# A hybrid decoder trunk: the first output projection by token tiles with resident weights, in place of block products

## The chip, the cores and the metric

The kernel runs on one core of one Trainium2 chip. The core has five engines that work side by side: TensorE (PE, with its weight loads as PEld), VectorE (DVE), ScalarE (ACT), GpSimd (POOL) and SyncE (SP, which here issues every DMA). The metric is the device time of one execution in microseconds (us), lower is better.

## The reference

Two layers on x of 2048 tokens by 1024 features, all float32. What matters here is the end of the first layer and the start of the second:

```python
def rmsnorm(x, g):
    y = x * lax.rsqrt(jnp.mean(x * x, axis=-1, keepdims=True) + RMS_EPS)
    return y * g

# layer 0, its end: eight heads (four softmax with forgetting, four stick-breaking)
mixed = concatenate([fox, sb], axis=-1) * silu(gate)      # 2048 x 1024
x1 = x + mixed @ even_w_out                               # 1024 x 1024 weights
# layer 1, its start
h = rmsnorm(x1, odd_norm)
proj = h @ odd_w_in                                       # q, k, v of three head groups, gate
```

`mixed @ even_w_out` is the first output projection. Layer 1 goes on with windowed attention in three groups of strides and a second output projection (`out = x1 + mixed1 @ odd_w_out`), which the change doesn't touch.

## The kernel before

Every product keeps nearly float32 accuracy by splitting both operands into a high half (rounded) and a low half, and by three matmuls: high by high, high by low, low by high (`mm3`, lines 88 to 93). The helper `split` makes the halves: high by a copy on ACT (line 81), low by a subtraction on DVE or POOL (line 86).

The large projections run as **block products** (`panel_steps`, line 261): for a panel of 512 columns and a half of the tokens (1024), the operands are cut into 2 by 2 blocks of 512, and seven products of sums of blocks take the place of eight products of blocks. One product is 48 matmuls of 128x256, in two halves, each with its own weight tile `wop`. `Weights` (line 184) makes these tiles a little ahead: it loads `wraw` (line 216), forms the block sums on POOL (line 226), and splits them (pool `wp`, 4 buffers). `left` (line 342) makes the seven left operands A11, A12, S2, S3, S1, A22, S4 of a token half from a transposed matrix in DRAM (`stage` and `lp` tiles, sums on DVE and POOL at line 345, splits); they live in the pool `big`, 8 buffers of 16 KB per partition. The results of the products are combined on DVE (line 300) and given to an `emit` function.

In the first output projection, four panels (two token halves by two column halves) are done so, from `mixT` (the transposed output of the attention). Its `emit` is `residual` (line 947): it loads a piece of x, adds (line 954), and stores to `x1d` in DRAM. Then, tile by tile (128 tokens), `transpose_to` (line 153) loads x1 again (`xt`), normalises it on ACT (squares at 131, scale at 133, with the small root steps at lines 104 to 114), transposes it on PE (line 142, 8 matmuls), scales by the norm's weights while copying out of PSUM (`te`, line 149, ACT), and stores to `hT1`, from which `left` makes the operands of layer 1. Transposes of the first token half are spread over the products of the second half, those of the second half over the first panels of layer 1 (`tick`).

The order of instructions on each engine isn't written out by hand: a scheduler orders them by priority (the order in which the program issues them) and by when it expects operands and buffers to be there. Each engine, and SP with its DMAs, then works through its queue in that order and stops at the first instruction whose operands aren't ready. The attention of layer 0 ends with eight units of 256 queries of the last head; a function `tail` is called between them, so that early work of the next stage can be laid beside them.

Of the kernel before, what the change touches and what calls it, by code (L numbers as in the profile page):

```python
# [8 lines left out]
F32 = mybir.dt.float32  # L9
# [551 lines left out]
def each(emit):  # L561

    def run(block, half, cs):
        for g, c in enumerate(cs):
            emit(block, half, g, c)
    return run
# [200 lines left out]
def even_attention(k, tail):  # L767
# [135 lines left out]
    for n, (kind, h, u) in enumerate(units):  # L903
# [20 lines left out]
        if nxt == len(order) and u in (5, 6):  # L924

            tail()
    for v in past:
        merged((pv(*v[0], v[1]), 1))


def odd_layer(k, x, x1, even_w_out, w_in, w_out, out):
# [4 lines left out]
    outs = [(even_w_out, plain(n * CH)) for n in range(2)]  # L936
    rounds = [[(n, g) for g in gs for n in "qkv"] + [("gate", 0)] for gs in ((1, 0, 2), (2, 1, 0))]
    cols = lambda n, g: plain(3 * 1536 if n == "gate" else "qkv".index(n) * 1536 + g * 512)
    W = Weights(k, outs * 2 + [(w_in, cols(*j)) for js in rounds for j in js],
                [2, 2] + [2, 1, 1, 1, 1, 1, 1, 1, 1] * 2)  # L940
    A = []
    lefts = left(k, k.mixT, 0, A)
    yield W, lefts

    tick = Pace()

    def residual(r, n):
        def emit(block, half, g, src):
            t0 = r * ROUND + block * CH + g * 256
            c0 = n * CH + half * 256  # L950
            view = lambda d: d[t0:t0 + 256, c0:c0 + 256].rearrange("(r p) c -> p r c", p=P)
            a = c2([P, 2, 256], name="x1t")
            nc.sync.dma_start(a, view(x))
            nc.vector.tensor_tensor(a, src.rearrange("p (r c) -> p r c", r=2), a, op=OP.add)
            nc.sync.dma_start(view(x1), a)
        return each(emit)
# [11 lines left out]

    for r in range(2):
        B = []  # L970
        nxt = left(k, k.mixT, 1, B) if r == 0 else left(k, T, 0, B)
        if r == 0:
            pace = Pace()
            pace.every = 2
            pace.add(lefts)
        both = two(A, [residual(r, n) for n in range(2)], pace if r == 0 else tick,
                   lambda j: None if j in EARLY else next(nxt))
        next(both)
        if r == 0:
            pace.finish()  # L980
            next(nxt)
            next(nxt)
        next(both)
        if r == 1:
            tick.finish()
            next(nxt)
            next(nxt)
        next(both)
        A = B
        tick.every = 1 if r == 0 else 4  # L990
        tick.add(iter("-"), staggered([k.transpose_to(T, x1, r * 8 + t, k.go) for t in (4, 5, 6, 7, 0, 1, 2, 3)]))
# [33 lines left out]

    box = k.big([P, 4, HG, 2, P], F32R, name="box")
    bias = box[:, 0].bitcast(F32)
    values = [box[:, 3].bitcast(F32).rearrange("p a b c -> p (a b c)")[:, i * HW:(i + 1) * HW] for i in range(4)]
    values += [k.hs.tile([P, HW], F32, name=f"v{i}") for i in range(2)]
    ring = box[:, 1:3].rearrange("p x a b c -> p (x a b c)").rearrange("p (z h s t) -> p z h s t", z=2, h=2, s=4)  # L1030
    pairs = box[:, 1:3].rearrange("p x a b c -> p (x a b c)").rearrange("p (z s h e t) -> p z s h e t", z=2, s=2, h=2, e=2)
# [153 lines left out]
    for r in range(2):  # L1185
        B = []
        nxt = left(k, T, 1, B, False)
        for i, (name, grp) in enumerate(rounds[r]):
# [11 lines left out]
            if i < 2:  # L1200
                if i == 0:
                    both = two(A, [emitter(r, *rounds[r][n]) for n in range(2)], beat)
                    next(both)
                next(both)
            else:
                panel(k, A, W, "t", emitter(r, name, grp), beat, (lambda j: next(nxt)) if last else None)
            if r == 0 and i == 2:
                tick.finish()
# [88 lines left out]
def tile_hybrid_trunk(ctx, tc, x, even_norm, even_w_in, even_b_f, even_q_gain, even_k_gain, even_w_out,  # L1297
# [12 lines left out]
    W, first = next(odd)  # L1310

    def tail():
        W.ahead(1)
        next(first)

    even_attention(k, tail)
    k.table()
# [29 lines left out]
```

## Time and profile before

| what | value |
|---|---|
| time, median of 3 runs | 2823.95 us (2823.14 to 2828.58) |
| the profiled execution's own time | 2826.53 us |
| its span in the trace | 2824.8 us |
| granted TensorE clock, mean | 0.979 |
| busy share of PE, DVE, ACT, POOL | 95%, 73%, 57%, 43% |
| last score product of layer 0's attention | 1283.0 us |
| matmuls of the projection, first to last start | 1297.4 to 1507.15 us |
| first matmul of layer 1's first panel | 1517.77 us |

In rows of groups the columns are: line, engine, operation, output<-inputs, shapes, count, then busy us, mean ns of one, and the idle time of the engine just before them with what ended it. Rows of the timeline give the start and the length in us, and in brackets the idle time before and its releaser. Lengths of matmuls include their pipeline, so that the step from start to start is the price of one. Rows of waits give the total in us, the number of times and the longest.

### The profile page before, as it was taken

Reading aid. Unit: us, or ns where it says so; the run is one execution under the profiler, and the core shown is the slowest. Engines: PE = TensorE matmul, PEld = TensorE weight load, DVE = VectorE, ACT = ScalarE, POOL = GpSimd, SP = SyncE. Lnnn points to the kernel's source line nnn. Section 1 sums busy time; section 2 is a strip of 40 time slices with the busy share of each in tenths; the row PEclk is TensorE's granted clock in tenths of the full one; section 3 lists DMA queues with packets and bytes.
Section 4 is the critical chain, followed back from the end, with each engine's and each line's share of the span. In section 5 each row is a group of like instructions: output and inputs, shape, how many; then the busy total and the mean of one; then the engine's idle time right before and its main releaser. Section 6 shows DMA issues by size and latency. Waiting matters only on the chain.

```text
span 2824.8 us, 55621 instructions
## 1 busy us (share of the span) xinstructions
PE 2676.4 (95%) x20191; PEld 2455.5 (87%) x20191; DVE 2052.7 (73%) x4373; ACT 1618.6 (57%) x3924; POOL 1223.4 (43%) x981
## 2 busy tenths in 40 slices
PE   6999999999999999998987999999989999999998
PEld 5898878998787789987887999999889999999876
DVE  7857684684888888888959857476797686763966
ACT  6465553454776666665364555555664577665642
POOL 3545464544544433326545544343245432422322
PEclk9999999999999999999998999999999999999999
DMA  5576544445433344435577553334543445444675
GB/s 180 181 222 210 172 160 154 154 142 192 144 111 118 112 123 144 139 104 173 187 232 246 154 179 107 121 122 146 169 128 126 139 140 166 132 147 134 219 254 183
DMA packets 398770, 449.43 MB, mean 159 GB/s; under 512 B 31712, under 2 KB 331040, under 8 KB 398496
## 3 DMA queue, kind: packets, MB, share of 16 engines
q1 hardware_dynamic: 398496, 445.89, 49.4%
q8 instruction: 159, 2.61, 0.4%
q14 instruction: 115, 0.94, 0.1%
HBM read 291.22 MB, written 154.57 MB: 158 GB/s over the span
## 4 chain that ended last, share of the span: by engine, by line
PE 62%; DVE 21%; DMA 7%; ACT 5%; issue 3%; POOL 1%; SPq 1%; DVEq 0%; ACTq 0%; POOLq 0%
PE ps L91 17%; PE ps L93 17%; PE ps L92 17%; DVE rest L828 4%; PE ps L863 2%; PE ps L1145 2%; DVE wop L86 2%; DVE A L86 2%; PE ps L1135 2%; PE ps L1116 2%; DVE lp L345 1%; DVE S L86 1%; PE ps L1061 1%; DVE pT L86 1%; DVE c L300 1%
## 5 line engine op out<-in xcount | busy, mean ns | idle before, releaser
L226 POOL TENSOR_TENSOR wraw<-wraw 128x512 f32<-128x512 f32 (+1 forms) x320 | 444.2, 1400 | 430.3 <-DVE wop L86 157.1
L81 ACT ACTIVATE wop<-wraw 128x512 fp32r<-128x512 f32 (+1 forms) x560 | 349.5, 629 | 383.4 <-PE ps L93 294.2
L86 POOL TENSOR_TENSOR wop<-wraw,wop 128x512 fp32r<-128x512 f32 (+1 forms) x240 | 329.4, 1375 | 534.0 <-ACT wop L81 503.8
L92 PE MATMUL ps<-wop,S 128*128 128x256 f32 (+1 forms) x1792 | 512.4, 286 | 18.1 <-DVE wop L86 16.8
L91 PE MATMUL ps<-wop,A 128*128 128x256 f32 (+1 forms) x1792 | 512.0, 287 | 14.2 <-DVE c L300 13.5
L91 PE MATMUL ps<-wop,S 128*128 128x256 f32 (+1 forms) x1792 | 515.8, 289 | 9.9 <-DVE c L300 6.3
L92 PE MATMUL ps<-wop,A 128*128 128x256 f32 (+1 forms) x1792 | 511.7, 286 | 2.2 <-DVE wop L86 1.5
L93 PE MATMUL ps<-wop,S 128*128 128x256 f32 (+1 forms) x1792 | 512.9, 287 | 0.0
L93 PE MATMUL ps<-wop,A 128*128 128x256 f32 (+1 forms) x1792 | 509.5, 285 | 0.0
L86 DVE TENSOR_TENSOR wop<-wraw,wop 128x512 fp32r<-128x512 f32 (+1 forms) x320 | 270.2, 845 | 232.0 <-ACT wop L81 230.6
L92 PEld LDWEIGHTS ps<-wop,S 128*128 128x128 f32 x1792 | 343.3, 192 | 21.0 <-DVE wop L86 17.8
L91 PEld LDWEIGHTS ps<-wop,A 128*128 128x128 f32 x1792 | 342.3, 191 | 19.0 <-issue 13.4
L91 PEld LDWEIGHTS ps<-wop,S 128*128 128x128 f32 x1792 | 342.1, 191 | 15.1 <-issue 8.4
L92 PEld LDWEIGHTS ps<-wop,A 128*128 128x128 f32 x1792 | 342.9, 191 | 4.0 <-DVE wop L86 3.2
L93 PEld LDWEIGHTS ps<-wop,S 128*128 128x128 f32 x1792 | 342.7, 191 | 3.3 <-issue 2.6
L93 PEld LDWEIGHTS ps<-wop,A 128*128 128x128 f32 x1792 | 342.7, 191 | 1.4 <-issue 0.8
L300 DVE TENSOR_TENSOR c<-u,ps 128x512 f32<-128x512 f32 (+1 forms) x274 | 178.7, 659 | 91.9 <-PE ps L93 86.1
L81 ACT ACTIVATE pT<-ps 128x512 fp32r<-128x512 f32 (+2 forms) x352 | 165.5, 504 | 135.6 <-PE ps L863 81.3
L831 POOL TENSOR_TENSOR rows<-rows,rest 128x512 f32<-128x512 f32 (+4 forms) x160 | 152.6, 957 | 162.1 <-DVE rest L828 141.8
L86 DVE TENSOR_TENSOR pT<-ps,pT 128x512 fp32r<-128x512 f32 (+2 forms) x352 | 188.0, 559 | 44.2 <-ACT pT L81 42.8
L1128 ACT ACTIVATE row<-row,nm 128x256 f32<-128x256 f32 (+1 forms) x384 | 172.5, 452 | 64.4 <-DVE nm L1126 63.9
L92 PE MATMUL ps<-pT,vt 128*128 128x256 f32 x576 | 171.1, 299 | 5.5 <-DVE pT L86 5.3
(214 smaller groups left out, 6485.0 us busy)
## 6 DMA issues: line engine op xcount, KB each, us to landing
wraw<-in_odd_w_in_dram SPq DMA_DIRECT2D x88, 512.0 KB, 4.0
wraw<-in_even_w_in_dram SPq DMA_DIRECT2D x70, 512.0 KB, 4.2
ld<-qk SPq DMA_DIRECT2D x106, 256.0 KB, 3.2
qk<-c SPq DMA_DIRECT2D x96, 256.0 KB, 2.4
lp<-hT SPq DMA_DIRECT2D x60, 256.0 KB, 3.6
uu<-ot SPq DMA_DIRECT2D x96, 132.0 KB, 1.9
fin<-uu SPq DMA_DIRECT2D x16, 792.0 KB, 4.5
hT<-te SPq DMA_DIRECT2D x48, 256.0 KB, 4.3
```

Source lines behind the costliest of these rows:

```text
L81: nc.scalar.activation(hi, src, AF.Copy)
L86: (nc.vector if lo_on == "dve" else nc.gpsimd).tensor_tensor(lo, src, hi.bitcast(F32), op=OP.subtract)
L91: mm(out, a[0], b[0], start=start, stop=False, skip_group_check=more)
L92: mm(out, a[0], b[1], start=False, stop=False, skip_group_check=more)
L93: mm(out, a[1], b[0], start=False, stop=stop, skip_group_check=more)
L226: tt = lambda e, o, x, y, op, s: e.tensor_tensor(o[:, s], x[:, s], y[:, s], op=op)
L300: nc.vector.tensor_tensor(out[g], x[g], y[g], op=OP.add)
L828: nc.vector.tensor_tensor_scan(o[:, b:b + n][:, ::-1], back, k.ident[:, :1].to_broadcast([P, n]), 1.0 if carry is None else carry, OP.mult ...
L831: nc.gpsimd.tensor_tensor(dst[:, :w], dst[:, :w], o[:, b + 1:b + 1 + w], op=OP.mult)
L863: nc.tensor.transpose(pt[:, (jx * 2 + i) * P:(jx * 2 + i + 1) * P], rows[:, i, (jj * 2 + jx) * P:(jj * 2 + jx + 1) * P], k.ident)
L1116: nc.tensor.matmul(scores(hp, e), q[pr, za, hp], ring[pr, zb, hp, blocks], start=i == 0, stop=i == 2)
L1128: nc.scalar.activation(row[:, h // 2, h % 2, :nk], row[:, h // 2, h % 2, :nk], AF.Exp, bias=nm[:, h:h + 1], accum_out=ot[:, HW + HG + h:HW ...
```

## The change

The first output projection no longer uses block products. A new function `first_out` keeps all of `even_w_out` on the chip as halves: four tiles `wo` in the pool `big`, loaded before the attention and split between the last units of its last head. It then takes pairs of token tiles from `mixT`, splits them (`ml`, also in `big`), and goes through 16 token tiles one by one: load x (`xt`), for each column half 8 x 3 matmuls of 128x512 into one PSUM bank and the sum with x in place, store to x1, normalise the same tile in place, transpose, store to `hT1`. Three tiles are in flight in a stagger. x1 is no longer read back for the norm. The left operands of layer 1's first half are begun near the end of the tiles (steps 13 and 14); the rest of them is issued with layer 1's first products. `box`, a tile of layer 1's attention, is made later, since its buffer isn't free before. `k.table()` behind the attention is gone.

```diff
-        if nxt == len(order) and u in (5, 6):
+        if nxt == len(order) and u in (3, 4, 5, 7):
             tail()
     for v in past:
         merged((pv(*v[0], v[1]), 1))
+        tail()
+
+def first_out(k, x, x1, w, T, W, lefts):
+    nc = k.nc
+    wo, raws, ml = {}, {}, {}
+    quarters = [(n, z) for n in range(2) for z in range(2)]
+
+    def load(i):
+        n, z = quarters[i]
+        raws[i] = [k.raws.tile([P, 2, CH], F32, name="wraw", tag="raw") for _ in range(2)]
+        for j, raw in enumerate(raws[i]):
+            k0 = (z * 4 + j * 2) * P
+            nc.sync.dma_start(raw, w[k0:k0 + 2 * P, n * CH:(n + 1) * CH].rearrange("(k p) n -> p k n", p=P))
+
+    def quarter(i):
+        t = wo[quarters[i]] = k.big([P, 4, 2, CH], F32R, name="wo")
+        for j, raw in enumerate(raws.pop(i)):
+            k.split(t[:, 2 * j:2 * j + 2, 0], t[:, 2 * j:2 * j + 2, 1], raw, "act", "dve")
+
+    def mixed(b):
+        t = ml[b] = k.big([P, KT, 2, 2 * P], F32R, name="ml")
+        for j in range(4):
+            c = k.c2([P, 2, 2 * P], name="mp", tag="res")
+            nc.sync.dma_start(c, k.mixT[:, 2 * j:2 * j + 2, b * 2 * P:(b + 1) * 2 * P])
+            k.split(t[:, 2 * j:2 * j + 2, 0], t[:, 2 * j:2 * j + 2, 1], c, "act", "dve")
+
+    def rows(t):
+        xt = k.w4([P, D], name="xt")
+        nc.sync.dma_start(xt, x[t * P:(t + 1) * P, :])
+        yield
+        m, i = ml[t // 2], slice(t % 2 * P, (t % 2 + 1) * P)
+        for n in range(2):
+            acc = k.ps("s")
+            for kk in range(KT):
+                k.mm3(acc, [m[:, kk, z, i] for z in range(2)],
+                      [wo[n, kk // 4][:, kk % 4, z] for z in range(2)], kk == 0, kk == KT - 1)
+            half = xt[:, n * CH:(n + 1) * CH]
+            nc.vector.tensor_tensor(half, acc, half, op=OP.add)
+        nc.sync.dma_start(x1[t * P:(t + 1) * P, :], xt)
+        k.normalise(xt)
+        yield
+        k.transposed(xt, k.go, lambda z: k.c2([P, 4, P], name="te"),
+                     lambda z, d: nc.sync.dma_start(T[:, z * 4:(z + 1) * 4, t * P:(t + 1) * P], d))
...
+    steps = staggered(rows(t) for t in range(NTT))
...
+    for s in range(NTT + 2):
+        next(steps, None)
+        if s in (2, 4, 6, 8, 10, 12):
+            mixed(s // 2 + 1)
+        if s == 9:
+            W.ahead(1)
+        if s in (13, 14):
+            next(lefts)
...
-    W = Weights(k, outs * 2 + [(w_in, cols(*j)) for js in rounds for j in js],
-                [2, 2] + [2, 1, 1, 1, 1, 1, 1, 1, 1] * 2)
+    W = Weights(k, [(w_in, cols(*j)) for js in rounds for j in js], [2, 1, 1, 1, 1, 1, 1, 1, 1] * 2)
     A = []
-    lefts = left(k, k.mixT, 0, A)
-    yield W, lefts
+    lefts = left(k, T, 0, A)
+    yield from first_out(k, x, x1, even_w_out, T, W, lefts)
     tick = Pace()
+    tick.add(lefts)
...
-        both = two(A, [residual(r, n) for n in range(2)], pace if r == 0 else tick,
-                   lambda j: None if j in EARLY else next(nxt))
...
-        tick.add(iter("-"), staggered([k.transpose_to(T, x1, r * 8 + t, k.go) for t in (4, 5, 6, 7, 0, 1, 2, 3)]))
```

The scheduler orders anew around the change. On PE, at the end of the attention (`ps<-pT,vt` is its value product, `ps<-ident,rows` its transposes), the order before is:

```order
L863 MATMUL ps<-ident,rows 128x128 x13
L91 MATMUL ps<-pT,vt 128x256
L91 MATMUL ps<-wop,A_14733 128x256
L92 MATMUL ps<-wop,A_14733 128x256
L93 MATMUL ps<-wop,A_14733 128x256
```

and now, at the same place:

```order
L863 MATMUL ps<-ident,rows 128x128 x9
L91 MATMUL ps<-pT,vt 128x128
L91 MATMUL ps<-pT,vt 128x256
L91 MATMUL ps<-wo,ml 128x512
L92 MATMUL ps<-wo,ml 128x512
```

In both, matmuls of the projection stand among the last value products; now they are those of the first two token tiles. On PE at the start of layer 1, the order before goes from the last block product of the projection straight to layer 1's first operand (`A_17358` is A11 of layer 1), with the tile transposes elsewhere:

```order
L91 MATMUL ps<-wop,S_16413 128x256
L92 MATMUL ps<-wop,S_16413 128x256
L93 MATMUL ps<-wop,S_16413 128x256
L91 MATMUL ps<-wop,A_17358 128x256
L92 MATMUL ps<-wop,A_17358 128x256
```

Now the last token tile is followed by the same product, with the transposes of tile 14 one matmul behind its start:

```order
L92 MATMUL ps<-wo,ml 128x512
L93 MATMUL ps<-wo,ml 128x512
L91 MATMUL ps<-wop,A_16626 128x256
L142 MATMUL ps<-ident,xt 128x128 x8
L92 MATMUL ps<-wop,A_16626 128x256
```

Those of each earlier tile stand a whole tile's matmuls behind its own, those of tile 15 at the end of the third product of layer 1. On DVE at that place, layer 1's operands stood before among residual adds (L954), block sums (L300) and weight halves:

```order
L86 TENSOR_TENSOR S_17538<-stage,S_17538 128x512 x2
L954 TENSOR_TENSOR x1t<-c,x1t 128x512
L300 TENSOR_TENSOR c<-u_17376,ps 128x512
L954 TENSOR_TENSOR x1t<-c,x1t 128x512
L345 TENSOR_TENSOR lp<-lp,stage 128x512
L954 TENSOR_TENSOR x1t<-c,x1t 128x512
L345 TENSOR_TENSOR lp<-lp 128x512
L300 TENSOR_TENSOR c<-u,ps 128x512 x2
L86 TENSOR_TENSOR S_17677<-lp,S_17677 128x512
```

Now they stand about the two sums of the last tile (L972), with the first weight half and the first block sum behind them:

```order
L86 TENSOR_TENSOR S_16986<-lp,S_16986 128x512
L86 TENSOR_TENSOR S_17054<-stage,S_17054 128x512 x4
L345 TENSOR_TENSOR lp<-lp 128x512
L86 TENSOR_TENSOR S_17123<-lp,S_17123 128x512 x2
L972 TENSOR_TENSOR xt<-ps,xt 128x512
L86 TENSOR_TENSOR S_17123<-lp,S_17123 128x512
L86 TENSOR_TENSOR A_17124<-lp,A_17124 128x512 x3
L86 TENSOR_TENSOR S_17222<-stage,S_17222 128x512 x4
L104 TENSOR_SCALAR ms<-ssx 128x1
L86 TENSOR_TENSOR wop<-wraw,wop 128x2x256
```

(`S_16986` is S2 of layer 1, `S_17054` S3, `S_17123` S1, `A_17124` A22, `S_17222` S4.) From about the fifth panel of layer 1 on, the order of every engine's work is that of before.

More of the change, by code (lines that the diff above doesn't have):

```diff
@@ L928, in even_attention @@
         merged((pv(*v[0], v[1]), 1))
+        tail()
[36 more added lines that the diff above has]
+                     lambda z, d: nc.sync.dma_start(T[:, z * 4:(z + 1) * 4, t * P:(t + 1) * P], d))
+    load(0)
+    load(1)
+    for i in range(4):
+        yield
+        quarter(i)
+        if i < 2:
+            load(i + 2)
+    steps = staggered(rows(t) for t in range(NTT))
+    for b in range(2):
+        yield
+        mixed(b)
+    yield
+    for s in range(NTT + 2):
[6 more added lines that the diff above has]
+            next(lefts)
@@ L935, in odd_layer @@
     plain = lambda c0: [[(c0, 256)], [(c0 + 256, 256)]]
-    outs = [(even_w_out, plain(n * CH)) for n in range(2)]
     rounds = [[(n, g) for g in gs for n in "qkv"] + [("gate", 0)] for gs in ((1, 0, 2), (2, 1, 0))]
     cols = lambda n, g: plain(3 * 1536 if n == "gate" else "qkv".index(n) * 1536 + g * 512)
-    W = Weights(k, outs * 2 + [(w_in, cols(*j)) for js in rounds for j in js],
-                [2, 2] + [2, 1, 1, 1, 1, 1, 1, 1, 1] * 2)
+    W = Weights(k, [(w_in, cols(*j)) for js in rounds for j in js], [2, 1, 1, 1, 1, 1, 1, 1, 1] * 2)
     A = []
-    lefts = left(k, k.mixT, 0, A)
-    yield W, lefts
+    lefts = left(k, T, 0, A)
+    yield from first_out(k, x, x1, even_w_out, T, W, lefts)
     tick = Pace()
[L947 to L956, printed above, removed]
+    tick.add(lefts)
     def two(A, emits, tick, after=None):
@@ L967, in two @@
             yield
[L969 to L975, printed above, removed]
-        both = two(A, [residual(r, n) for n in range(2)], pace if r == 0 else tick,
-                   lambda j: None if j in EARLY else next(nxt))
[L978 to L990, printed above, removed]
-        tick.add(iter("-"), staggered([k.transpose_to(T, x1, r * 8 + t, k.go) for t in (4, 5, 6, 7, 0, 1, 2, 3)]))
     qk = [dr.tile([S, 2, 2, HW], F32, name=f"qk{g}") for g in range(3)]
@@ L1023, in emitter @@
         return emit
[L1026 to L1031, printed above, removed]
     turn, cleared = [0], []
@@ L1203, in odd_layer @@
                     next(both)
+                    if r == 0:
+                        tick.finish()
+                        box = k.big([P, 4, HG, 2, P], F32R, name="box")
+                        bias = box[:, 0].bitcast(F32)
+                        values = [box[:, 3].bitcast(F32).rearrange("p a b c -> p (a b c)")[:, i * HW:(i + 1) * HW] for i in range(4)]
+                        values += [k.hs.tile([P, HW], F32, name=f"v{i}") for i in range(2)]
+                        ring = box[:, 1:3].rearrange("p x a b c -> p (x a b c)").rearrange("p (z h s t) -> p z h s t", z=2, h=2, s=4)
+                        pairs = box[:, 1:3].rearrange("p x a b c -> p (x a b c)").rearrange("p (z s h e t) -> p z s h e t", z=2, s=2, h=2, e=2)
                 next(both)
@@ L1309, in tile_hybrid_trunk @@
     odd = odd_layer(k, x[0], x1, even_w_out[0], odd_w_in[0], odd_w_out[0], out[0])
[L1310 to L1317, printed above, removed]
+    next(odd)
+    even_attention(k, lambda: next(odd))
     next(odd, None)
```

2 lines of the change are left out of this document (removed).

## The prediction

> **What bounds the kernel now.** I read the page's first two parts, then the timeline of PE around the projection, the waits of PE there, and the busy time by stage. The page first:
>
> ```profile
> PE 2676.4 (95%) x20191; PEld 2455.5 (87%) x20191; DVE 2052.7 (73%) x4373; ACT 1618.6 (57%) x3924; POOL 1223.4 (43%) x981
> PE   6999999999999999998987999999989999999998
> PEclk9999999999999999999998999999999999999999
> ```
>
> PE is full in nearly every slice except a few about the middle (the 19th to 22nd, some 1270 to 1550 us), which is where the changed stage lies. Four rows of PE's timeline fix it:
>
> ```profile
> 1283.42 0.62 PE L863 MATMUL ps<-ident,rows 128*128 128x128 f32 x4
> 1507.15 0.28 PE L93 MATMUL ps<-wop,S 128*128 128x256 f32 x1
> 1517.77 0.55 PE L91 MATMUL ps<-wop,A 128*128 128x256 f32 x1 [10.34 <-DVE c L300]
> 1618.71 1.04 PE L142 MATMUL ps<-ident,xt 128*128 128x128 f32 x8
> ```
>
> The last score product of the attention has been issued at 1283.4; the last product of the projection at 1507.2; then PE idles 10.34 us; from 1517.8 to 1618.7 run the first two panels of the second layer (2 x 7 block products). I call 1283.4 to 1618.7 the stretch: 335.3 us. Behind it PE has no idle time to speak of, and the instruction order soon becomes the same as before, so what the stretch gains, the end gains.
>
> ```profile
> 1283.40:1310.50 27.10, 24.05 (x188) 23.20 (x186) 17.52 (x37) 16.70 (x33) 16.05 (x12) 0.94 0.41 122
> 1310.50:1404.70 94.20, 77.78 (x627) 76.28 (x627) 88.52 (x98) 36.90 (x66) 61.70 (x39) 0.95 0.63 202
> 1404.70:1517.70 113.00, 93.73 (x737) 91.93 (x735) 76.55 (x123) 65.34 (x157) 53.66 (x37) 0.92 0.75 246
> 1517.70:1618.70 101.00, 89.52 (x696) 88.73 (x697) 89.65 (x144) 52.17 (x118) 63.44 (x43) 0.91 0.55 175
> 1618.70:1680.00 61.30, 61.30 (x522) 61.30 (x521) 29.38 (x60) 36.57 (x92) 28.75 (x22) 1.00 0.62 190
> ```
>
> These are windows; the columns are length, then PE, PEld, DVE, ACT, POOL busy, the granted clock, DMA share and GB/s. In the first half of the projection DVE is busy 88.5 of 94.2 us and PE only 77.8: DVE sets the pace. The same holds at the start of the second layer (89.7 of 101). The waits of PE in the stretch agree:
>
> ```profile
> PE ps L92 <- DVE wop L86: 18.3, 7, 8.4
> PE ps L91 <- DVE c L300: 16.6, 3, 10.3
> PE ps L142 <- ACT xt L133: 6.8, 3, 2.9
> PE ps L863 <- POOL rows L847: 2.9, 2, 1.9
> ```
>
> With the smaller rows of that view (5.8 us together) PE idles 50.4 us here.
>
> **The prices.** Block products are 128x256 matmuls, the new ones 128x512; the second form runs in the last projection of the program.
>
> ```profile
> 1501.59 0.28 PE L91 MATMUL ps<-wop,S 128*128 128x256 f32 x1
> 1523.00 0.28 PE L91 MATMUL ps<-wop,A 128*128 128x256 f32 x1
> 2797.48 0.39 PE L91 MATMUL ps<-wof,mhl 128*128 128x512 f32 x1
> 2807.10 0.39 PE L93 MATMUL ps<-wof,mhl 128*128 128x512 f32 x1
> 1447.74 1.04 PE L142 MATMUL ps<-ident,xt 128*128 128x128 f32 x8
> 1448.54 0.36 PE L93 MATMUL ps<-wop,S 128*128 128x256 f32 x1
> ```
>
> A product's 48 matmuls start between 1501.59 and 1507.15: 5.56 us / 47 = 0.118 us each. Between 2797.48 and 2807.10 lie 42 steps: 0.229 us for a 128x512. Eight transposes of one token tile take 1448.54 - 1447.74 = 0.8 us. After the gap of 10.34 us the first 24 matmuls take from 1517.77 to 1523.00, 0.218 us each, while windows with gaps show a granted clock of 0.91 to 0.95: a gap of that size costs another 24 x 0.1 = 2.4 us behind itself.
>
> [...]
>
> **The change part by part.** *Products removed:* 2 token halves x 2 column panels x 7 products x 48 = 1344 matmuls x 0.118 = 158.6 us of PE. *Products added:* 16 token tiles x 2 column halves x 8 row blocks x 3 = 768 x 0.229 = 175.9 us. So PE itself has 17.3 us more to do: 8 products where there were 7, a little repaired by the wider form.
>
> *Feeding work removed.* Rows of the stretch, and of ACT from 1404.7 to 1517.7:
>
> ```profile
> L86 DVE TENSOR_TENSOR wop<-wraw,wop 128x512 fp32r<-128x512 f32 x49 | 45.2, 925 | 11.0 <-ACT wop L81 10.9
> L954 DVE TENSOR_TENSOR x1t<-c,x1t 128x512 f32<-128x512 f32 x32 | 31.8, 998 | 9.0 <-DMA x1t<-in_x_dram 8.9
> L300 DVE TENSOR_TENSOR c<-u,ps 128x512 f32<-128x512 f32 x46 | 30.8, 678 | 3.0 <-ACT u L305 1.9 <-PE ps L93 0.9
> L86 DVE TENSOR_TENSOR A<-stage,A 128x512 fp32r<-128x512 f32 x16 | 15.6, 1015 | 0.0
> L149 ACT ACTIVATE te<-ps,go 128x128 f32<-128x128 f32 x64 | 17.6, 380 | 1.7 <-PE ps L142 1.7
> L133 ACT ACTIVATE xt<-xt,r 128x1024 f32<-128x1024 f32 x8 | 9.0, 1148 | 11.1 <-DVE r L114 11.1
> L131 ACT ACTIVATE junk<-xt 128x1024 bf16<-128x1024 f32 x8 | 8.5, 1060 | 4.6 <-DMA xt<-x1d 4.6
> L108 ACT ACTIVATE r<-lg 128x1 f32<-128x1 f32 x8 | 1.7, 226 | 0.0
> L81 ACT ACTIVATE S<-stage 128x512 fp32r<-128x512 f32 x7 | 3.9, 618 | 0.2 <-DVE stage L345 0.2
> L111 DVE TENSOR_TENSOR t<-t,ms 128x1 f32<-128x1 f32 x12 | 7.2, 603 | 0.2
> L157 SPq DMA_DIRECT2D xt<-x1d x16: 319/412/477, 1409.8 to 1635.8; - x16
> ```
>
> On DVE go the low halves of the weight blocks (4 panels x 8 = 32 x 0.925 = 29.6 us), the block sums (4 panels x 12 = 48 x 0.678 = 32.5), and the low halves of two sets of seven left operands (56 x about 1.0 = 56, a fifth of it already ahead of 1283). POOL loses 4 panels x 8 weight sums. Added on DVE: 32 low halves of the token operands, of which I price each at 0.68 to 1.0 (22 to 32 us), and eight double-size ones of the weights, run inside the attention where they replace the early left operands of before. The residual add remains 32 times, but now takes one operand from PSUM like L300 (0.678). Sum: 118 + 10 us less, about 27 more: DVE is left with some 170 us in the stretch against 272 before. It no longer sets the pace of the projection; PE does.
>
> *A tile's turn.* A tile holds PE 48 x 0.229 + 0.8 = 11.8 us. ACT has for it 1.06 + 0.2 (squares), 0.4 (the two root steps), 1.15 (scale), 8 x 17.6/64 = 2.2 (transposes out), half of a pair's four splits at 0.63 (1.3): 6.3 us, beside PE. The chain from a tile's last matmul to its transposes is about 0.4 + 0.7 + 1.3 + 0.4 + 1.2 and five small DVE operations of at most 0.6: some 6 us; if it queues behind the neighbour's transposes (2.2) and a pair's splits (2.5), 10.7 us. PE's order puts a whole tile, 11.0 us of matmuls, between: covered, by little in the worst case. If that cover went, each us of lateness would cost up to 16 us. DMAs shrink: SP drops the second reading of x1 (16 loads) and 32 small residual loads and stores for 16 and 16 large ones, and per tile issues 6, each about 0.4 us.
>
> *The seam.* The second layer's first operands depend on the first eight tiles alone, which are out five tiles ahead. PE goes on with the next layer's product behind tile 15 (order shown above), so the 10.34 us gap has no cause left. S2 to S4 need buffers that the projection's weights free at its end; their 16 to 20 splits lie beside the four first products, 4 x 5.7 = 22.7 us: 20 x 0.68 = 13.6 us of DVE if alone, 20 x 1.0 = 20 with POOL beside it. Eight tile transposes that lay among the next panels move into the projection (two of them just past its end).
>
> **The sum.** Three rows like the first of these hold the rest of the attention's value products in the stretch, 92 in all, 8 of them half as wide; the second holds its transposes:
>
> ```profile
> L92 PE MATMUL ps<-pT,vt 128*128 128x256 f32 (+1 forms) x31 | 9.2, 295 | 0.2 <-DVE pT L86 0.2
> L863 PE MATMUL ps<-ident,rows 128*128 128x128 f32 x46 | 8.3, 315 | 2.9 <-POOL rows L847 2.9
> ```
>
> The stretch of after, in PE time: rest of attention 84 x 0.118 + 8 x 0.06 + 46 x 0.1 = 15.0; projection 175.9; 16 x 0.8 = 12.8 transposes; two panels 672 x 0.118 = 79.3. Together 283.0 us. Before: 335.3, and 5 of the 16 tile transposes lay behind the stretch (4.0): 339.3. What stays lost: in the attention's end 3 us (before 2.9 of idle and a cold stretch; POOL has no left sums there any more); in the projection 3 (bounds 0 and 12, one late us per tile in most tiles); in the two panels before lost 101.0 - 79.3 - 3 x 0.8 = 19.3 us, of which I keep 8:
>
> ```profile
> 1550.12 0.58 PE L92 MATMUL ps<-wop,S 128*128 128x256 f32 x1 [4.54 <-DVE wop L86]
> 1592.60 0.55 PE L91 MATMUL ps<-wop,S 128*128 128x256 f32 x1 [5.12 <-DVE c L300]
> ```
>
> The first gap came with DVE behind on residual adds and left operands, which go; the second lies in the norms of the panels themselves and stays, with the 2.4 to 2.9 us behind it (bounds 0 and 19.3). So 283.0 + 14 = 297.0, a gain of 42.3 us. The profiled execution took 2826.53 us (span 2824.8, 1.7 outside): 2784.2. It is 2.6 us above the median, 2823.95, from which it would be 2781.7. I say **2783 us**; with all bounds at their good end 283.0 (2770), at their bad end 283.0 + 3 + 12 + 19.3 = 317.3 (2804.5).
>
> **Rivals.**
> 1. *DVE at the seam* (20 of 100): S2 to S4 come too late, since their buffers come free only with the last tile. Then the 10.3 us gap and the 19.3 us of before stay: 283.0 + 6 + 29.6 = 318.6, **2806 us**. For it: DVE 89.65 of 101, and the splits 1.015 us where POOL works beside them; against: the residual adds and the small work of eight tiles are gone there. [...]
> 2. *The tile chain* (7 of 100), the case on the other side: transposes or the PSUM sums of a tile aren't ready when PE comes to them, for ACT, DVE and SP serve everything in order and one blocked head holds all. Place: each of 16 tiles; it is slower than before once a tile's chain exceeds its 11.0 us by 42.3/16 = 2.6. With a chain of 15 us: 16 x 4 = 64 us, **2848 us**. Against: my worst sum is 10.7.
> 3. *Nothing lost* (7 of 100): 283.0, **2770 us**.
> 4. *The wait only moves to the token operands*: load, ACT half and DVE half of a pair's four pieces come late by 42.3/8 = 5.3 us for each of the 8 pairs, and the eighth product is paid for nothing: no change, about **2825 us** (2 of 100). Against it: a pair needs 4 x 0.63 on ACT and 4 x 1.0 on DVE, side by side, while PE has 23.6 us of work on the pair before.
> 5. *The 128x512 matmul runs faster in this loop than in the last projection* (1 of 100): at half of 0.229 the sum falls by 88 us, to 2695. [...]
>
> **How the numbers follow.** The forecast (own range 2774 to 2796) has 63 of 100. The range 2768 to 2808 leaves out rival 2 and the ends of 3 and 4. A difference of 0.2% is about 5.6 us, what this kernel's runs can tell. Faster: 63 + 20 + 7 + 1 = 91; same 2; slower 7.
>
> **What would show it.** Right: PE between 1285 and 1590 busy over 93% with a clock of 0.97 or more; 768 matmuls of wo by ml about 0.23 us apart; the second layer's first product some 22 to 26 us earlier (1492 to 1496) with no gap ahead; DVE under 65% in the projection. Wrong: waits of PE on xt (ACT L133) or on the sums of line 972 in every tile (rival 2); a gap above 5 us on S2 or S3 (rival 1); a spacing above 0.24; waits on the halves of line 86 (rival 4).

## The result, and the profile after

The changed kernel takes 2783.93 us (median of four runs, 2782.93 to 2786.42). The kernel before, run beside it, takes 2826.26 us (median of four, 2823.14 to 2828.89). The ratio is 0.9852, with a 95% interval from 0.9835 to 0.9869: 42 us less. The prediction said 2783 us. The profiled execution of the changed kernel took 2782.93 us, span 2781.2, against 2826.53 and 2824.8 before.

The page of the changed kernel, the rows that stand ahead of the prediction for the kernel before (busy time by engine, PE in 40 slices) and the chain that ended last, by engine:

```profile
PE 2672.4 (96%) x19615; PEld 2423.1 (87%) x19615; DVE 1935.3 (70%) x4257; ACT 1579.9 (57%) x3843; POOL 1105.8 (40%) x905
PE   6999999999999999999999999999989999999998
PE 72%; DVE 17%; ACT 4%; DMA 3%; issue 2%; POOL 1%; SPq 0%; DVEq 0%; ACTq 0%; POOLq 0%
```

The dent of the 19th to 22nd slice is gone, and PE holds 72% of the chain (62% before). PE is no busier in sum than before (2676.4 us then): the 42 us are idle and slow time that went, not work. By the prediction's prices the stretch before held 261.7 us of matmuls (15.0 + 158.6 + 11 x 0.8 + 79.3) in 335.3 us, so 73.6 us were lost: 50.4 of them idle, the rest in slower steps (the granted clock was 0.92 there).

The same stretch by stage, changed kernel; columns as before: length, then PE, PEld, DVE, ACT and POOL busy, granted clock, DMA share, GB/s. The first row is the attention's end with the whole projection, the second the second layer's first two panels:

```profile
1283.90:1490.20 206.30, 204.25 (x1026) 172.49 (x1025) 87.14 (x194) 105.53 (x260) 21.74 (x15) 1.00 0.57 182
1490.20:1581.80 91.60, 85.12 (x689) 84.58 (x688) 72.93 (x114) 40.69 (x89) 54.16 (x40) 0.96 0.40 124
```

These two are the prediction's stretch: 206.3 + 91.6 = 297.9 us, where 297.0 was predicted and 335.3 (339.3 with the five transposes behind it) was measured before. With 283.0 us of matmuls in it, 14.9 us are lost now. PE is busy 99% of the first at full clock, and VectorE (DVE) 87 of 206 us. PE's timeline at the places of the prediction, changed kernel:

```profile
1295.37 0.39 PE L91 MATMUL ps<-wo,ml 128*128 128x512 f32 x1
1466.61 1.03 PE L142 MATMUL ps<-ident,xt 128*128 128x128 f32 x8
1490.16 0.28 PE L91 MATMUL ps<-wop,A 128*128 128x256 f32 x1
1544.51 0.36 PE L91 MATMUL ps<-wop,S 128*128 128x256 f32 x1 [1.24 <-DVE c L300]
1550.15 0.39 PE L92 MATMUL ps<-wop,S 128*128 128x256 f32 x1 [2.41 <-DVE wop L86]
1557.48 0.36 PE L91 MATMUL ps<-wop,S 128*128 128x256 f32 x1 [2.83 <-DVE c L300]
1581.81 0.28 PE L91 MATMUL ps<-wop,A 128*128 128x256 f32 x1
```

The projection's first matmul is at 1295.37, and the second layer's first product follows the projection at 1490.16 with nothing idle ahead of it; before it stood at 1517.77 behind the gap of 10.34 us. What still idles lies in the two panels. All waits of PE from 1270 to 1600, changed kernel (total us, times, longest):

```profile
PE ps L91 <- DVE c L300: 4.1, 2, 2.8
PE ps L92 <- DVE wop L86: 2.4, 1, 2.4
PE ps L92 <- DVE nm L836: 1.6, 1, 1.6
PE ps L92 <- DVE pT L86: 0.4, 1, 0.4
```

That is 8.5 us where the kernel before had 50.4, and none of it is in a token tile.

The second layer's first attention work (transposes of line 1061 before, line 1088 now) starts 1680.03 - 1638.71 = 41.3 us earlier. The spans differ by 43.6; the other 2.3 us arise later in this pair of executions and were not followed up. By the medians the gain is 42.3.

### The profile page after: what moved, and what is told of

It is laid out like the page before. It is cut to its first block, busy times and chain, and to the rows that moved or that the text cites. A ratio compares the mean times of both kernels' runs of the same rounds, so it can differ in the third digit from the quotient of the medians.

```text
span 2781.2 us, 53979 instructions
## 1 busy us (share of the span) xinstructions
PE 2672.4 (96%) x19615; PEld 2423.1 (87%) x19615; DVE 1935.3 (70%) x4257; ACT 1579.9 (57%) x3843; POOL 1105.8 (40%) x905
## 4 chain that ended last, share of the span: by engine, by line
PE 72%; DVE 17%; ACT 4%; DMA 3%; issue 2%; POOL 1%; SPq 0%; DVEq 0%; ACTq 0%; POOLq 0%
PE ps L91 20%; PE ps L93 20%; PE ps L92 19%; DVE rest L828 4%; PE ps L863 3%; PE ps L1172 2%; PE ps L1162 2%; PE ps L1143 2%; DVE pT L86 1%; PE ps L1088 1%; DVE wop L86 1%; DVE A L86 1%; DVE lp L345 1%; DVE c L300 1%; PE ps L1135 1%
## 5 line engine op out<-in xcount | busy, mean ns | idle before, releaser
L226 POOL TENSOR_TENSOR wraw<-wraw 128x512 f32<-128x512 f32 (+1 forms) x288 | 396.4, 1387 | 422.6 <-DVE wop L86 156.1
L81 ACT ACTIVATE wop<-wraw 128x512 fp32r<-128x512 f32 (+1 forms) x504 | 316.3, 631 | 351.4 <-PE ps L93 281.8
L86 POOL TENSOR_TENSOR wop<-wraw,wop 128x512 fp32r<-128x512 f32 (+1 forms) x216 | 290.6, 1348 | 504.4 <-ACT wop L81 490.9
L91 PE MATMUL ps<-wop,A 128*128 128x256 f32 (+1 forms) x1600 | 456.2, 286 | 4.1 <-DVE c L300 3.0
L92 PE MATMUL ps<-wop,A 128*128 128x256 f32 (+1 forms) x1600 | 455.9, 285 | 0.0
L93 PE MATMUL ps<-wop,A 128*128 128x256 f32 (+1 forms) x1600 | 453.7, 284 | 0.0
L91 PE MATMUL ps<-wop,S 128*128 128x256 f32 (+1 forms) x1536 | 442.3, 288 | 4.1 <-DVE c L300 4.1
L92 PE MATMUL ps<-wop,S 128*128 128x256 f32 (+1 forms) x1536 | 437.4, 285 | 2.4 <-DVE wop L86 2.4
L93 PE MATMUL ps<-wop,S 128*128 128x256 f32 (+1 forms) x1536 | 438.1, 285 | 0.0
L86 DVE TENSOR_TENSOR wop<-wraw,wop 128x512 fp32r<-128x512 f32 (+1 forms) x288 | 236.6, 822 | 233.1 <-ACT wop L81 228.4
L91 PEld LDWEIGHTS ps<-wop,A 128*128 128x128 f32 x1600 | 303.6, 190 | 8.5 <-DVE c L300 3.5
L93 PEld LDWEIGHTS ps<-wop,A 128*128 128x128 f32 x1600 | 304.5, 190 | 1.4 <-issue 0.8
L92 PEld LDWEIGHTS ps<-wop,A 128*128 128x128 f32 x1600 | 304.5, 190 | 1.2 <-issue 0.5
L91 PEld LDWEIGHTS ps<-wop,S 128*128 128x128 f32 x1536 | 291.2, 190 | 8.4 <-issue 5.9
L92 PEld LDWEIGHTS ps<-wop,S 128*128 128x128 f32 x1536 | 291.7, 190 | 4.1 <-DVE wop L86 2.6
L93 PEld LDWEIGHTS ps<-wop,S 128*128 128x128 f32 x1536 | 291.7, 190 | 3.2 <-issue 2.6
L300 DVE TENSOR_TENSOR c<-u,ps 128x512 f32<-128x512 f32 (+1 forms) x242 | 157.4, 656 | 90.4 <-PE ps L93 83.6
```

The costliest lines, as they stand in the source:

```text
L81: nc.scalar.activation(hi, src, AF.Copy)
L86: (nc.vector if lo_on == "dve" else nc.gpsimd).tensor_tensor(lo, src, hi.bitcast(F32), op=OP.subtract)
L91: mm(out, a[0], b[0], start=start, stop=False, skip_group_check=more)
L92: mm(out, a[0], b[1], start=False, stop=False, skip_group_check=more)
L93: mm(out, a[1], b[0], start=False, stop=stop, skip_group_check=more)
L226: tt = lambda e, o, x, y, op, s: e.tensor_tensor(o[:, s], x[:, s], y[:, s], op=op)
```

## The experiments

**Does TensorE set the pace of the projection now?** Three variants of the changed kernel ask this. The first makes TensorE's part a little longer:

```diff
-                k.mm3(acc, [m[:, kk, z, i] for z in range(2)],
-                      [wo[n, kk // 4][:, kk % 4, z] for z in range(2)], kk == 0, kk == KT - 1)
+                for p in range(2):
+                    cols = slice(p * 256, (p + 1) * 256)
+                    k.mm3(acc[:, cols], [m[:, kk, z, i] for z in range(2)],
+                          [wo[n, kk // 4][:, kk % 4, z, cols] for z in range(2)], ...)
```

> The changed kernel with each 128x512 matmul of the token tiles issued as two 128x256 ones (1536 matmuls in place of 768, same products, same order of tiles). Theory (TensorE sets the pace of the new projection): 1536 x 0.118 = 181.2 us against 768 x 0.229 = 175.9 us, so 5 us slower than the changed kernel, about 2789; the matmuls still run without gaps. Rival (the work that feeds TensorE, on VectorE and ScalarE, sets the pace): those few us vanish in waits that are there anyway, 0 us, about 2784.

Measured: 2792.67 us (median of four), 8.7 over the changed kernel. In PE's timeline of this variant a tile's turn goes from one group of transposes to the next:

```profile
1474.37 1.03 PE L142 MATMUL ps<-ident,xt 128*128 128x128 f32 x8
1486.75 1.04 PE L142 MATMUL ps<-ident,xt 128*128 128x128 f32 x8
```

12.38 us a tile. In the changed kernel the two tiles' turns between the transposes at 1466.61 and the projection's end at 1490.16 take 23.55, so 11.78 each; 16 x 0.60 = 9.7 us. PE has no wait in a tile here either. The theory holds; its 5 us were too few because the step of 0.118 us was read in the block products, while here a tile's 96 matmuls take 12.38 - 0.79 = 11.59 us, 0.121 each. The wide ones take 0.229 as predicted (21.97 us for 96, with two groups of transposes of 0.79 taken off). Why the narrow step is a little longer here was not followed up.

The second gives VectorE more to do:

```diff
             k.split(t[:, 2 * j:2 * j + 2, 0], t[:, 2 * j:2 * j + 2, 1], c, "act", "dve")
+            for _ in range(2):
+                nc.vector.tensor_tensor(t[:, 2 * j:2 * j + 2, 1], c, t[:, 2 * j:2 * j + 2, 0].bitcast(F32), op=OP.subtract)
```

> The changed kernel with the low halves of the token operands computed three times over, the same subtraction of 128x512 each time (64 more instructions, at 0.68 to 1.0 us each 43 to 64 us more of VectorE in the projection of some 206 us). Theory (VectorE is no longer the bound there, it is busy below 65%): hidden, 0 to 4 us over the changed kernel. Rival (VectorE still sets the pace): the whole 43 us or more appear, about 2827 or later.

Measured: 2788.05 us, 4.1 over the changed kernel. VectorE's busy time rose by 38.9 us (1974.2 against 1935.3), so nine tenths of it are hidden. From the last value product of the attention to the end of the projection, this variant:

```profile
1321.70:1494.70 173.00, 173.00 (x821) 144.34 (x820) 87.69 (x191) 88.37 (x225) 15.03 (x11) 1.00 0.61 196
```

PE is busy all 173 us although VectorE is now at half. The 4 us arise ahead of that, in the attention's end, where PE waits 2.6 us (0.4 in the changed kernel) for the probabilities' low halves, which queue behind the added work on VectorE. There, VectorE's cover is thin; in the tiles it is not.

The third takes work from TensorE:

```diff
-                k.mm3(acc, [m[:, kk, z, i] for z in range(2)],
-                      [wo[n, kk // 4][:, kk % 4, z] for z in range(2)], kk == 0, kk == KT - 1)
+                for z in range(2):
+                    nc.tensor.matmul(acc, m[:, kk, 0, i], wo[n, kk // 4][:, kk % 4, z], start=kk == z == 0, stop=...)
```

> The changed kernel, leaving out of every three matmuls of the projection the one with the low half of the tokens (512 left of 768, 256 x 0.229 = 58.6 us less of TensorE; the projection's result is that much less exact); everything that feeds them is still computed. Theory (TensorE alone sets the pace): a tile then holds TensorE 7.3 + 0.8 = 8.1 us, still over the 6.3 of ScalarE, so 45 to 58 us faster than the changed kernel, about 2726 to 2739; less where the tiles' chain of 6 to 11 us no longer fits under 7.3 us of matmuls, which would then show as waits on the transposes' input. Rival (the feeding work sets the pace): under 15 us faster.

Measured: 2733.25 us (median of four), 50.7 under the changed kernel for 58.6 us less of TensorE. The projection ends 54.0 us earlier (1436.14 against 1490.16). The two stages, and the one new long wait:

```profile
1300.00:1436.00 136.00, 134.63 (x683) 113.39 (x683) 65.14 (x154) 88.22 (x225) 14.97 (x10) 1.00 0.75 244
1452.52 0.58 PE L92 MATMUL ps<-wop,A 128*128 128x256 f32 x1 [4.71 <-DVE wop L86]
```

TensorE stays full in the tiles even at two thirds of its work. What is given back lies behind the projection, where the second layer's weight blocks are now late by 4.7 us. So TensorE sets the pace of the projection; and with the projection 54 us shorter, the cover that the seam has in the changed kernel is used up.

**How near is the tiles' chain?** The rival on the slower side was the chain from a tile's last matmul to its transposes. This variant makes it longer without work for any engine:

```diff
         nc.sync.dma_start(x1[t * P:(t + 1) * P, :], xt)
+        nc.sync.dma_start(xt, x1[t * P:(t + 1) * P, :])
         k.normalise(xt)
```

> The changed kernel, but each token tile is read back from x1 in DRAM, after it was stored there, before it is normalised, as the kernel before did. The chain from a tile's last matmul to its transposes grows by a store and a load (together some 7 to 9 us by the loads of the trace), no engine has more to compute. Theory (a tile has about 11 us of cover and a chain of some 6): 13 to 15 us of chain against 11 of cover; if the order of TensorE stays, 2 to 4 us late in each of 16 tiles, 30 to 60 us slower; if the instruction order is set a tile later by the program's planner, 0 to 10 us. Rival (the gain comes from dropping the second reading of x1): most of the 42 us are gone, whatever the order of TensorE.

Measured: 2800.72 us (median of four), 16.8 over the changed kernel. PE's waits from 1320 to 1502 in this variant have one row of any size:

```profile
PE ps L142 <- ACT xt L133: 7.7, 6, 3.6
```

The store and the load take 3.2 and 3.4 us from issue to landing here. The longer chain shows as waits on the transposes' input in six tiles, and the projection ends 11.9 us later (1502.05 against 1490.16), of which these waits are 7.7; the rest is lost in the two panels behind it, where PE waits 12.7 us against 6.5. The number falls between the theory's two cases, 30 to 60 us and 0 to 10, and the rival's (most of the 42 us gone) is out: with the second reading of x1 put back, 26.9 of the 42 us are still there (2827.59 of the kernel before beside it, less 2800.72).

The changed kernel's own chain can be read in one tile. VectorE's second sum, ScalarE's scaling, and the transposes:

```profile
1384.29 0.69 DVE L972 TENSOR_TENSOR xt<-ps,xt 128x512 f32<-128x512 f32 x1 [4.49 <-PE ps L93]
1389.26 1.15 ACT L133 ACTIVATE xt<-xt,r 128x1024 f32<-128x1024 f32 x1 [0.81 <-DVE r L114]
1395.89 1.03 PE L142 MATMUL ps<-ident,xt 128*128 128x128 f32 x8
```

From 1384.29 to 1390.41 are 6.1 us (predicted: some 6), and the transposes come 5.5 us later.

**Is the gap at the seam gone because of what the operands depend on?** The left operand of the second layer's first half is loaded from the last eight tiles instead of the first eight:

```diff
-    lefts = left(k, T, 0, A)
+    lefts = left(k, T, 1, A)
```

> The changed kernel, with one thing altered in the second layer: the left operand of its first half is loaded from tokens 1024 to 2047 instead of 0 to 1023 (so both halves compute on the same tokens), which the projection finishes last. Theory (the 10.3 us gap of before at the seam is gone because the second layer's first operands depend on the first eight tiles alone, out long before): now the first operands wait for the last tiles, a chain of store, load, split and sums; the gap returns, 10 to 30 us of idle TensorE and the cold matmuls behind it, 12 to 35 us slower than the changed kernel, 2796 to 2819. Rival (the gap went with VectorE's load, whatever the operands depend on): under 4 us.

Measured: 2812.68 us (median of four), 28.8 over the changed kernel. The projection ends at the same place (1491.26). Behind it, the waits of PE from 1491 to 1610 and the window:

```profile
PE ps L93 <- DVE S L86: 10.7, 4, 7.0
PE ps L91 <- ACT S L81: 8.7, 4, 3.5
PE ps L91 <- DVE u L300: 5.3, 1, 5.3
1491.00:1610.00 119.00, 94.22 (x694) 92.14 (x693) 99.66 (x135) 47.93 (x103) 73.46 (x49) 0.86 0.40 126
```

24.7 us of idle, with the clock down to 0.86, and VectorE at 99.7 of 119 us: the wait at the seam is back, and two thirds of what the change gained are lost (28.8 of 42.3).

**What was it, then, that bound the kernel before?** The prediction said VectorE. Three variants of the kernel before test it. In the first the addition of x is left out:

```diff
-            nc.vector.tensor_tensor(a, src.rearrange("p (r c) -> p r c", r=2), a, op=OP.add)
-            nc.sync.dma_start(view(x1), a)
+            nc.sync.dma_start(view(x1), src.rearrange("p (r c) -> p r c", r=2))
```

> The kernel before with one part left out: the addition of x to the first layer's projection (32 VectorE instructions, 31.8 us by the prediction's row of line 954; x is still read, and x1 is the projection alone, so the later layer computes on other numbers). Theory (in the kernel before, VectorE sets the pace of the block products of this projection, not TensorE): most of the 32 us of VectorE come off the stretch, 10 to 25 us faster than the kernel before, 2802 to 2817, with the gaps ahead of the projection's products smaller. Rival (TensorE or the transfers set the pace there, and the change gains by something else, the dropped second reading or the order): under 4 us.

Measured: 2818.96 us (median of ten; the kernel before beside it 2826.78), 7.8 us faster, ratio 0.9972 (0.9960 to 0.9984). VectorE's busy time over the execution fell by 35.9 us (2052.7 to 2016.8). The expectation of 10 to 25 missed, and so did the rival's "under 4". A second variant takes the second token half's left operands off, the third both:

```diff
-        B = []
-        nxt = left(k, k.mixT, 1, B) if r == 0 else left(k, T, 0, B)
+        B = A if r == 0 else []
+        nxt = iter("-" * 7) if r == 0 else left(k, T, 0, B)
```

> The kernel before with the seven left operands of the second token half left out: the second half's products reuse the operands of the first, so x1 is wrong there. This takes 28 low halves and 12 block sums off VectorE (28 x about 1.0 + 12 x about 0.9 = 39 us), and their loads, ScalarE halves and GpSimd sums with them. It follows on the run that freed VectorE of the residual addition and gained 8 us of 32. Theory now (the pace of before was set by the whole feeding of the block products, loads and block sums of the left operands in a chain over three engines, of which VectorE's time is only a part; freeing VectorE alone moves the wait to the loads): this gains much more per us of VectorE taken off than the residual did, 20 to 40 us, 2786 to 2806. Rival (VectorE's time alone counts, at the rate of the run before, a quarter): about 10 us, 2817.

> The kernel before with both left out, the residual addition and the left operands of the second token half. Theory (feeding as a whole sets the pace): the two together reach nearly all of the 51 us that TensorE lost in the projection: 35 to 50 us faster than the kernel before, 2776 to 2792, the products of the projection running with gaps of under 2 us. Rival (weight blocks and the seam set the pace): no more than 20 us.

Measured: 2814.12 us for the second (13.0 us under the 2827.14 of before) and 2809.49 us for the third (17.6 us). VectorE's busy time fell by 33.2 and 59.2 us. Both times are near the rivals' numbers, 10 and at most 20, and far below the theory's 20 to 40 and 35 to 50. The traces say why. In the third variant the middle of the projection is what the theory wanted, a window of 50 us without a gap:

```profile
1350.00:1400.00 50.00, 50.00 (x425) 50.00 (x424) 19.40 (x28) 11.39 (x18) 20.45 (x15) 1.00 0.47 156
```

But at its start and its end the long waits stand as before, on the same lines:

```profile
1341.12 0.58 PE L92 MATMUL ps<-wop,S 128*128 128x256 f32 x1 [10.26 <-DVE wop L86]
1500.38 0.55 PE L91 MATMUL ps<-wop,A 128*128 128x256 f32 x1 [8.11 <-DVE c L300]
```

Ahead of the second of them VectorE's timeline in the third variant reads:

```profile
1489.97 4.65 DVE L86 TENSOR_TENSOR A<-stage,A 128x512 fp32r<-128x512 f32 x4
1494.55 5.08 DVE L86 TENSOR_TENSOR S<-lp,S 128x512 fp32r<-128x512 f32 x3
1499.55 0.68 DVE L300 TENSOR_TENSOR c<-u,ps 128x512 f32<-128x512 f32 x1
```

Seven low halves of the second layer's left operands take 9.6 us, and the sum that PE waits for stands behind them. So what bound the kernel before was not VectorE's sum of work over the stage. It was bursts, each the left operands of one half. Two of them carry the long waits, those of the first half (8.35 us) and of the second layer (10.34 us), and none of the three variants removes these. The burst of the second half, which the second and third variants remove, cost PE five waits of 0.9 to 1.5 us between 1365 and 1385 in the kernel before, 6.4 us together; neither variant has a wait there. In the second variant a part is given back at once: PE reaches the first transposes of the tiles 7.41 us before their input. That the two long waits go with their bursts is read from the order on VectorE; no variant of the kernel before takes those operands away.

What a burst looks like is seen ahead of the first long wait of the kernel before: VectorE's timeline, GpSimd's below it, and PE's row:

```profile
1325.80 1.78 DVE L86 TENSOR_TENSOR A<-lp,A 128x512 fp32r<-128x512 f32 x1
1327.50 6.77 DVE L86 TENSOR_TENSOR S<-stage,S 128x512 fp32r<-128x512 f32 x4
1334.19 1.75 DVE L86 TENSOR_TENSOR S<-lp,S 128x512 fp32r<-128x512 f32 x1
1335.87 1.75 DVE L86 TENSOR_TENSOR A<-lp,A 128x512 fp32r<-128x512 f32 x1
1337.54 0.68 DVE L86 TENSOR_TENSOR wop<-wraw,wop 128x512 fp32r<-128x512 f32 x1
```

```profile
1328.66 1.72 POOL L345 TENSOR_TENSOR lp<-lp 128x512 f32<-128x512 f32 x1
1330.34 5.05 POOL L226 TENSOR_TENSOR wraw<-wraw 128x512 f32<-128x512 f32 x3
1335.36 1.71 POOL L86 TENSOR_TENSOR wop<-wraw,wop 128x512 fp32r<-128x512 f32 x1
```

```profile
1338.27 0.58 PE L92 MATMUL ps<-wop,S 128*128 128x256 f32 x1 [8.35 <-DVE wop L86]
```

Seven low halves of left operands take VectorE from 1325.80 to 1337.54, about 1.7 us each, while GpSimd works beside it; the low half of the one weight block that PE waits for comes behind them and takes 0.68. The additions of x lie spread among the products, so taking them away shortens few of the bursts (the first long wait is 10.14 us without them): 7.8 us for 35.9.

**Can the rest be had?** In the changed kernel the two panels still lose 10.7 us (91.6, less 79.3 of products and 1.6 of two transposes). They are the q and the k panel, whose heads are normalised on VectorE. In the next variant each group's v panel, which has no norms, comes first:

```diff
-    rounds = [[(n, g) for g in gs for n in "qkv"] + [("gate", 0)] for gs in ((1, 0, 2), (2, 1, 0))]
+    rounds = [[(n, g) for g in gs for n in "vqk"] + [("gate", 0)] for gs in ((1, 0, 2), (2, 1, 0))]
...
-            if name == "v":
+            if name == "k":
```

> The changed kernel with the second layer's column panels in the order v, q, k of each group instead of q, k, v (its attention is queued behind k). Computes the same. The first two panels then are v and q, of which v has no norms to compute on VectorE, ScalarE and GpSimd. Theory (the 10.7 us that are still lost in those two panels come from the norms of q and k, with VectorE busy 73 of 91.6 us there): 3 to 8 us faster, 2776 to 2781. Rival (they come from the operands and weights being readied there, or the norms of k only move into the next panel where they stall as much): 0, or slower by as much as the attention that now starts against another panel loses, up to 10 us.

Measured: 2780.45 us (median of four; 2778.89 to 2786.70), 3.5 under the changed kernel, not to be told from it by this run alone. The two panels of this variant:

```profile
1488.60:1570.00 81.40, 81.40 (x689) 81.39 (x688) 50.55 (x78) 35.42 (x75) 48.81 (x36) 1.00 0.47 143
```

81.4 us against 91.6, all of them busy: the 10 us are there, and VectorE's part fell from 72.9 to 50.6. Later the attention of line 1162 waits more for VectorE (9.1 us in all behind the two panels, where the changed kernel has 4.2), probably since each group's attention now starts right behind the norms of k. To test that, the order v, q, k was kept for the first group alone:

```diff
+    rounds[0][:3] = [("v", 1), ("q", 1), ("k", 1)]
...
-            if name == "v":
+            if i % 3 == 2:
```

> The changed kernel with the order v, q, k in the second layer's very first group of panels alone (all other groups q, k, v as in the changed kernel). Computes the same. In the run with v first in all groups the first two panels gained 10 us, of which 6 were lost again later by waits of the attention that starts behind the norms of k. Theory (those losses come from the later groups, whose attention starts against k's norms): most of the 10 us stay, 6 to 10 us faster than the changed kernel, 2774 to 2778. Rival (the loss comes from the first group's own attention, which starts later or against k's norms): as the run before, 3 to 4 us, 2780.

Measured: 2775.64 us (median of five), ratio to the kernel before 0.9818 (0.9805 to 0.9832), 8.3 under the changed kernel: the theory's 6 to 10. The waits of that line for VectorE are back at 3.9 us. To compare the two versions directly, both ran once more on one chip:

> The changed kernel as it is, beside the next one on the same chip, so that the two can be compared without the kernel before between them. Expected by all: 2784, as in its first runs.

> The version with v, q, k in the very first group, computes the same. Theory (10 us of waits and cold matmuls behind the norms of q and k in the second layer's first two panels are gone and stay gone): 6 to 10 us faster than the changed kernel beside it. Rival (the difference of the first runs was one of chips or of scatter): under 4 us.

Measured: 2783.60 us (2779.83 to 2785.98) for the changed kernel and 2774.78 us (2772.01 to 2777.04) for the other: 8.8 us, no run of the one among those of the other. The two panels of the faster one, in its first run:

```profile
1491.70:1573.20 81.50, 81.50 (x690) 81.46 (x689) 50.18 (x78) 35.80 (x75) 49.08 (x36) 1.00 0.47 143
```

This version computes the same as the changed kernel and is the fastest here of those that leave nothing out.

## Why the prediction was right, and where it was not

- **The prices.** The 128x512 matmul took 0.229 us in the tiles, the eight transposes 0.79. The first was the term that mattered, and it rested on rows of another stage of the same program; rival 5 (half of it) is out: no run shows a step of half that length, and the shortest between two of these matmuls in the changed kernel's tiles is 0.22. The narrow variant shows that the wide form gains 16 x 0.60 = 9.7 us in this loop; the sum's repair was 1536 x 0.118 - 175.9 = 5.3.
- **PE's sum.** Predicted 283.0 us of work and 14 lost, measured 297.9 in all; between 1285 and 1590 PE was busy 97% at a clock of 0.99 (over 93% and 0.97 expected). The attention's end and the projection lost 206.3 - 202.1 = 4.2 us (3 + 3 expected; 202.1 is 15.0 + 175.9 + 14 x 0.8), the two panels 10.7 (8 expected). The first term was a little high, the second a little low; that the sum is off by only 0.9 us is in part luck, since the two errors cancel. That the second is what is left of the gaps of 4.54 and 5.12 us was right; that having the norms of both panels there causes it is shown by the variant with v first, which has one panel's norms there and none of the gaps (the first two panels run interleaved, so both panels' norms fall into this window).
- **"VectorE sets the pace", of the kernel before.** This is the step that failed, as it was put. It was read from a busy share of 88.5 in 94.2 us. Taking 35.9 us off VectorE gave 7.8, taking off one burst and its sums (33.2 us) 13.0, both (59.2 us) 17.6; and in the third variant PE was full at a VectorE share of 39% between two bursts that held PE up for 10 and 8 us. The engine was right and the mechanism not: what set the pace was bursts, the operands of a half standing in VectorE's order ahead of a weight block's low half, or of the sums that PE waits for. The forecast did not suffer, since its sum is TensorE's own work and what stays lost and holds no price for a us of VectorE; and the change takes away the operand sets of both halves and moves the third off the seam. A smaller change, priced at so many us of VectorE saved, would have been forecast 2.6 to 4.6 times too well.
- **VectorE after the change.** Predicted some 170 us in the stretch, measured 87.1 + 72.9 = 160; in the projection 42% (under 65% expected). The prediction's list left out the block sums of the left operands (line 345 on VectorE: 25.6 us in the stretch before, 7.4 now). The 64 instructions that were added in the variant cost 4 us of 38.9.
- **A tile's chain.** Predicted about 6 us, measured 6.1, covered with 5.5 to spare. One part was not named: the scaling writes the tile in place, so it must wait until the tile's store to x1 has been read out. ScalarE's group of that line, changed kernel, from 1310 to 1490:

```profile
L133 ACT ACTIVATE xt<-xt,r 128x1024 f32<-128x1024 f32 x15 | 17.3, 1156 | 27.2 <-DVE r L114 15.7 <-DMA x1d<-xt 11.5
```

  11.5 us of ScalarE's idle time in 15 tiles end with that store. It costs nothing here, as PE waits for no tile. Rival 2 asked for chains of over 13.6 us; the variant with store and load in the chain, the same reading back as before, lost 16.8 us and remained well faster than the kernel before.
- **The seam.** Predicted: no gap, first product between 1492 and 1496. Measured: no gap, 1490.16, a little earlier still. The reason given (the operands hang on the first eight tiles alone) is shown by the variant that makes them hang on the last eight: 28.8 us. A wait at the place that rival 1 names is thus real, though from another cause; its own condition, buffers free only with the last tile, did not bind: VectorE is through with the low halves of S3 before the projection ends (the row at 1486.40 below). With the projection 54 us shorter there is a wait of 4.71 us behind the seam, but it is on a weight block's low half, so it doesn't show that condition either.
- **Rival 4** (waits on the token operands) has no row: PE waits for no `ml` half in any tile.

## What to carry to other kernels

Here a busy share near the full window (88.5 of 94.2 us) named the engine that was late, but not how much an instruction taken off it is worth: look at what stands in its queue ahead of the instruction that the waiting engine needs, and price the burst, not the sum. A stage that needs its operands a piece at a time, each piece feeding as much matmul work as it takes to make, can do more TensorE work (here 17 us more) and still end earlier than one that needs a whole set of operands at once. Where two stages meet, let the second one's first operands depend on the first one's early tiles (28.8 us here), and put work without a long tail of vector operations first (8.8 us here).

## What the runs showed of the hardware that was not expected

- **Two engines at one pace.** In the burst ahead of 1337.54 VectorE's low halves start 1.67 to 1.70 us apart, and GpSimd's instructions take 1.7 each in the same time. 4 in 6.77 us on the one side and 3 in 5.05 on the other is one pace; what ties them is not shown. At the changed kernel's seam, where GpSimd stands idle (14.64 us up to 1489.20), four such low halves take 2.50 us:

```profile
1486.40 2.50 DVE L86 TENSOR_TENSOR S<-stage,S 128x512 fp32r<-128x512 f32 x4
```

  At that pace the burst of seven would take some 4.4 us in place of 11.7, an estimate; no run takes GpSimd's work out of the burst to test it. The prediction priced them at 1.015, the mean over a window in which GpSimd worked a part of the time (194.9 of 335.3 us).
- **Behind a short gap the slow clock can come later, or not at all.** Behind the wait of 2.41 us in the changed kernel PE's timeline reads:

```profile
1550.97 0.39 PE L92 MATMUL ps<-wop,S 128*128 128x256 f32 x1
1551.16 0.41 PE L93 MATMUL ps<-wop,S 128*128 128x256 f32 x1
1554.36 0.30 PE L93 MATMUL ps<-wop,S 128*128 128x256 f32 x1
```

  From 1550.15 the first step is 0.23 us and those up to 1550.97 are 0.12, at a granted clock of 1.00; from 1550.97 to 1554.36 (3.39 us) they are 0.21, at 0.50: 16 matmuls, 1.5 us lost. Behind the wait of 1.24 us six us earlier the first step is 0.19 and the others are 0.12. In the variant that reads x1 back, the wait of 2.42 us at the same place (1567.67 there) has no slow step behind it but the first (0.22, then 0.11 to 0.12). In the variant with more work on VectorE a wait of 2.44 us, at the place of the one of 1.24 us, had none either (0.19, then 0.12), and the next one, of 2.41 us, had (0.21 for 3.39 us, from 1556.36). So the length of one gap does not decide. In the changed kernel a second stretch of 3.39 us at a clock of 0.50 begins 6.82 us after the first (1557.79), just behind the wait of 2.83 us. What decides is not shown by these runs.
